# Branch A of the first token block: key blocks of 72 (nine grid rows by eight columns) against key blocks of 128 (sixteen columns by eight rows), with the meta tokens placed apart

## The chip, the cores and the metric

The kernel runs on one core of a Trainium2 chip. The metric is the device time of one execution in microseconds (us). TensorE (PE) multiplies; its weight loads are listed apart as PEld. VectorE is DVE, ScalarE is ACT, GpSimd is POOL, and SyncE (SP) issues the transfers (DMAs).

## The reference, cut to what matters

One encoder layer is applied to two groups of tokens, one sequence of 2048 and one of 512, with 16 learned meta tokens ahead of each.

```
u = rms_norm(h)                                  # 1024 features
qa, ka, va, za, qb, kb, vb, zb, ga, gb = split(u @ w_in)
o_a = neighbourhood_attention(qa, ka, va)        # 8 heads of 64
o_b = window_attention(qb, kb, vb)               # 8 query heads, 2 key heads
y = sigmoid(ga) * ((o_a * silu(za)) @ w_proj_a) + sigmoid(gb) * ((o_b * silu(zb)) @ w_proj_b)
h = h + y @ w_out;  out = rms_norm(h) without the meta tokens
```

Branch A lays the tokens on a grid of 64 columns. The sequence of 512 tokens has 8 rows, so each of its tokens sees all 8 rows, 16 columns around its own, and the 16 meta tokens: 128 + 16 keys under one softmax. All arithmetic is to be as exact as 32-bit floats.

## The kernel before

A 32-bit operand is split in a high part (`h`, a rounded copy by ACT) and a low part (`l`, the rest, by DVE or POOL). A product takes three matmuls, high by high, high by low and low by high; the attention products take two.

**Stages.** The tokens lie in five windows of 512; window 0 is the short sequence, windows 1 to 4 are the long one. The first stage (0 to 126 us) projects window 4 and the meta tokens alone, feature block by feature block (`beside` and `alone`). In the second stage (from 126 us) and the third, two windows share one weight block by a scheme of seven products (`pairs`, `begin`, `sides_first`, `sides`). All projections go to DRAM. From about 990 us on come the attention units, with the remaining gate projections and the output products between them as filling work.

**A unit of branch A.** `unit_a(w, p, h, g)` is one window, one pair of heads, one head and one group of 16 query columns by 8 rows (128 queries). For window 0 a head has four units, g = 0 to 3, and there are eight heads, so 32 units. A unit sees 24 or 32 grid columns. Its keys are a row of meta tokens, written as a ninth row beside the 8 grid rows, so a score tile has 9 x 24 = 216 or 9 x 32 = 288 columns. The steps are: scores (L997, L998), bias and maximum on DVE (L935), exponentials with their sum on ACT (L942), reciprocal and scaling (L946, L953, or on ACT L951 for g = 1), transposes of blocks of 72 keys (8 columns by 9 rows) on PE (L1009), high part by ACT (L1012), low part by DVE (L1013), products with the values (L1024 high, L1026 low). `A_ORDER`, `A_FIRST` and `A_PRODUCTS` say which of the eight column blocks of a head are transposed in which unit and which product covers which groups of queries. A head has 3 + 4 + 4 + 3 = 14 transposes and 6 + 4 + 6 = 16 products, 12 of them over 256 query columns and 4 over 128.

**The values.** `put_v` stores the projected values, transposed, in `va_d`; `put_v_meta` stores those of the meta tokens, from the tile `vm`, in `vrow_d`, which is first filled with zeros. `vm` has one buffer (`bufs=1`). Both are called for the four pairs of heads in the first stage, `put_v_meta` there alone. `put_v` for window 0 runs in the second stage.

**What sets the order.** PE runs in the order in which the program is written, and SP too until the attention begins. On ACT, DVE and POOL a scheduler in the build chooses the order by a simulated timeline. Each engine then runs its list in order, so an instruction that waits holds up all behind it on that engine.

**Names of the second stage's start.** `begin` issues a product into the tile `pa` and one into `pc`; `pairs` then issues `product(a, x["p6"], u[2], False)`, again into `pa`, and `product(e, x["p5"], u[3], True)` into `pe`. The weights `p6` and `p5` are the two halves of a tile `wt` that `sides` makes from two freshly loaded weight tiles: DVE forms `s` (L724, L729, L725, L731), ACT writes the high half (L186) and DVE the low half (L187). `last_operands` splits the operands `u5` and `u6` (L360 on ACT, L361 on DVE). `tq` (L260) is the sum that is stored once `pc` is done.

Of the kernel before, what the change touches and what calls it, by code (L numbers as in the profile page):

```python
# [87 lines left out]
def encoder_block(ctx: ExitStack, tc: tile.TileContext, xT, x_end, w_in, w_pa, w_pb, w_o, norm_g, final_g,  # L88
# [6 lines left out]
    def dt(name, shape):  # L95
        return dram.tile(shape, F32, tag=name, name=name)
# [511 lines left out]
    def put_v(br, w, p, t):  # L608
        vn = ev.tile([P, 2, 4, P], F32R, tag="ev", name="vn")
        transposed(vn, t, 4, P)  # L610
        if br == "a":

            for x in range(2):
                dst = va_d[p][:, w * 64 : (w + 1) * 64, 4 * x : 4 * x + 4].rearrange("g p k f -> p g k f")
                move(dst, vn[64 * x : 64 * x + 64])
        else:
            move(vb_d[w * WTOK : (w + 1) * WTOK].rearrange("(c p) g f -> p g c f", p=P), vn)

    def put_v_meta(br, p, src):
        vm = st.tile([N_META, 2, 1, P], F32R, tag="vm", name="vm", bufs=1)  # L620
        transposed(vm, src, 1, N_META)
        if br == "a":
            if p == 0:
                zr = ev.tile([P, WTOK], F32, tag="t", name="zr", bufs=3)[:, :P]
                nc.vector.memset(zr, 0.0)
                for d in vrow_d:
                    move(d.rearrange("c b g f -> (c b g) f"), zr)
            n = len(META_COLS)
            for y in range(2):
                b = v_block(META_COLS[0] // 8 + y)  # L630
                move(vrow_d[p][:, b : b + n].rearrange("c b g f -> c b (g f)"),
                     vm[8 * y : 8 * y + 8].rearrange("m g o f -> m o (g f)").broadcast_to([8, n, 2 * P]))
        else:
            move(vbm_d, vm[:, :, 0])
# [303 lines left out]
    def sums_of():  # L938
        return at.tile([P, 2], F32, tag="sm", name="sm", bufs=8)
# [22 lines left out]
    def unit_a(w, p, h, g, sh):  # L962

        grows, i0, k0, kr = a_window(w)
        R = kr + 1
        kind = a_kind(w)
        t0 = (0 if w == 0 else DEC_SEQ) + k0 * GRID_W
        nt = kr * GRID_W
        c0, C = CG[g]
        n = R * C  # L970
        nb, kb = C // 8, R * 8
        hs = slice(64 * h, 64 * h + 64)
        qs = slice(g * P, (g + 1) * P)
        if g == 0 and h == 0:
            q = sh["q"] = ld.tile([P, 2, 2, WTOK], F32R, tag="q", name="q")
            move(q.rearrange("p h i t -> p h (i t)"), qa_d[w, p].rearrange("(h d) j x -> (d j) h x", h=2))
        if g == 0 and h == 1:
            z = sh["z"] = ld.tile([P, WTOK], F32, tag="z", name="z")
            move(z, z_d["a", w, p])
        if g == 0:  # L980
            kd = sh["kd"] = ld.tile([P, R, GRID_W], F32R, tag="kd", name="kd")
            move(kd[:, 1:, :].rearrange("p r c -> p (r c)"),
                 ka_d[p][hs].rearrange("d i t -> (d i) t")[:, t0 : t0 + nt])
            move(kd[:, 0, :], kam_d[p][hs].rearrange("d i t -> (d i) t"))
            v = sh["v"] = ld.tile([P, 8, P], F32R, tag="v", name="v", bufs=3)
            move(v[8:kb], va_d[p][h, t0 // 8 : t0 // 8 + kb - 8])
            move(v[:8], vrow_d[p][:, :, h])
            b = sh["b"] = ld.tile([P, a_kind_width(2)], F32, tag="ba", name="ba")
            move(b[:, : a_kind_width(kind)], bias_a[kind][2 * p + h])
        q, kd, v, z, bias = (sh.get(x) for x in ("q", "kd", "v", "z", "b"))  # L990
        yield
        if g == 0 and h == 0:
            sh["y"] = at.tile([P, WTOK], F32, tag="y32", name="y32")
        y32 = sh["y"]
        s = ps_s.tile([P, WTOK], F32, tag="s", name="s")
        sv = s[:, :n].rearrange("p (r c) -> p r c", r=R)
        nc.tensor.matmul(sv, q[:, h, 0, qs], kd[:, :, c0 : c0 + C], start=True, stop=False)  # L997
# [4 lines left out]
        sm = sums_of()[:, :1]  # L1002
        exps(pr[:, :n].rearrange("p (b r c) -> p r b c", b=nb, c=8), sv.rearrange("p r (b c) -> p r b c", c=8), nm, sm)
        yield
        normalise(pr[:, :n], inverse(sm), on_act=g == 1)
# [4 lines left out]
        a = slice(A_FIRST[g], A_FIRST[g] + 2 * nb - 1, 2)  # L1010
        tb = tp[:kb, : nb * P].rearrange("p (b t) -> p b t", t=P)
        nc.scalar.copy(ph_[:kb, a], tb)  # L1012
        nc.vector.tensor_sub(pl_[:kb, a], tb, f32(ph_[:kb, a]))  # L1013
# [4 lines left out]
        for i, (part, b, x, gs) in enumerate(A_PRODUCTS[g]):  # L1018
            vb = v[:kb, v_block(b), :]
            cols = slice(gs[0] * P, (gs[-1] + 1) * P)  # L1020
            src = (ph_ if part == "h" else pl_)[:kb, x : x + len(gs)].rearrange("p b t -> p (b t)")

            if part == "h":
                nc.tensor.matmul(o[:, cols], vb, src, start=g == 1 and i == 0, stop=False, skip_group_check=True)  # L1024
            else:
                nc.tensor.matmul(o[:64, cols], vb[:, :64], src, start=False, stop=(g, i) == (3, 5),  # L1026
                                 skip_group_check=True)
# [511 lines left out]
```

## Time and profile before

| what | us |
|---|---|
| three runs, median (lowest to highest) | 1918.04 (1917.67 to 1918.76) |
| profiled execution, its own time | 1917.62 |
| its span from the first to the last instruction | 1915.5 |
| time around the span | 2.1 |
| PE busy in the span | 1882.1 |
| DVE, ACT, POOL busy | 1313.5, 1143.5, 727.4 |

In the timeline a row gives the start, the duration, and in brackets the idle time before it with what ended it. A matmul's duration covers its way through the pipeline, so the pace of PE is read from one start to the next. ACT and DVE rows overlap by about 0.1 us in the same way. The four units of a head of window 0 return every 11.1 us.

### The profile page before, as it was taken

How to read it: one execution, taken by the hardware profiler on the slowest of the kernel's cores; microseconds unless marked ns; L12 is line 12 of the kernel's file. 1: busy time of each engine (PE TensorE's matmuls, PEld its weight loads, DVE VectorE, ACT ScalarE, POOL GpSimd, SP SyncE). 2: the span in 40 equal slices, each digit the busy share in tenths (PEclk: the TensorE clock that was granted, in tenths of full speed). 3: DMA queues.
4: the chain of work that ended last, by engine and by line, in shares of the span. 5: the costliest groups of instructions: out<-in, count | busy, mean ns of one | idle time of the engine just before them, and what ended most of it. 6: DMA issues, size and time to landing. Idle time of an engine off the chain costs nothing.

```text
span 1915.5 us, 29776 instructions
## 1 busy us (share of the span) xinstructions
PE 1882.1 (98%) x9925; PEld 1599.7 (84%) x9925; DVE 1313.5 (69%) x2899; ACT 1143.5 (60%) x2515; POOL 727.4 (38%) x556
## 2 busy tenths in 40 slices
PE   8999999999999999999999999999999999999998
PEld 6998888888878888888878888888888888888876
DVE  8886445556477544345457788878888887888874
ACT  6454444444464444444456787787788778778831
POOL 2005342323102222323223336646744864684320
PEclk9999999999999999999999999999999999999999
DMA  7667554644296775544369868977986996798482
GB/s 261 218 190 294 175 200 164 220 170 171 90 338 216 240 209 192 193 139 158 110 204 293 255 213 258 303 217 256 306 268 197 305 317 200 234 287 253 129 321 86
DMA packets 223761, 423.78 MB, mean 221 GB/s; under 512 B 49640, under 2 KB 90808, under 8 KB 222072
## 3 DMA queue, kind: packets, MB, share of 16 engines
q1 hardware_dynamic: 223320, 421.88, 67.1%
q8 instruction: 79, 1.29, 0.3%
q14 instruction: 74, 0.61, 0.1%
q10 hardware_dynamic: 288, 0.01, 0.0%
HBM read 303.07 MB, written 118.74 MB: 220 GB/s over the span
## 4 chain that ended last, share of the span: by engine, by line
PE 82%; DVE 5%; ACT 5%; DMA 4%; issue 2%; POOL 1%; SPq 0%; ACTq 0%; DVEq 0%; POOLq 0%
PE pa L758 23%; PE pe L758 11%; PE pc L758 6%; PE mm L137 3%; PE mm L135 3%; PE mm L136 3%; PE tp L1009 3%; PE pso L137 3%; PE pso L135 3%; PE pso L136 2%; PE tp L1109 2%; PE psb L136 2%; PE psb L137 1%; PE oa L1026 1%; PE psb L135 1%
## 5 line engine op out<-in xcount | busy, mean ns | idle before, releaser
L187 POOL TENSOR_TENSOR wt<-wraw,wt 128x512 fp32r<-128x512 f32 x164 | 213.8, 1323 | 271.5 <-ACT wt L186 260.9
L758 PE MATMUL pa<-u,wt 128*128 128x512 f32 x1008 | 242.9, 390 | 0.0
L758 PE MATMUL pa<-u,x 128*128 128x512 f32 x984 | 237.8, 390 | 0.0
L758 PEld LDWEIGHTS pa<-u,wt 128*128 128x128 f32 x1008 | 188.7, 188 | 39.0
L758 PEld LDWEIGHTS pa<-u,x 128*128 128x128 f32 x984 | 183.8, 188 | 38.1
L186 ACT CAST wt<-wraw 128x512 fp32r<-128x512 f32 x312 | 177.6, 618 | 54.9 <-PE mm L137 31.4
L729 POOL TENSOR_TENSOR s<-wraw,raw 128x512 f32<-128x512 f32 x40 | 57.9, 1446 | 273.9 <-DVE x L187 273.9
L135 PE MATMUL mm<-u,wt 128*128 128x512 f32 (+2 forms) x416 | 151.7, 365 | 8.3 <-ACT u L313 7.2
L724 POOL TENSOR_TENSOR s<-raw 128x512 f32<-128x512 f32 x40 | 58.6, 1466 | 255.1 <-DMA raw<-in_w_in_dram 137.6
L137 PE MATMUL mm<-u,wt 128*128 128x512 f32 (+2 forms) x416 | 148.0, 356 | 2.6 <-DVE wt L187 2.0
L136 PE MATMUL mm<-u,wt 128*128 128x512 f32 (+2 forms) x416 | 147.5, 354 | 0.0
L187 DVE TENSOR_TENSOR wt<-wraw,wt 128x512 fp32r<-128x512 f32 x148 | 103.5, 738 | 52.8 <-ACT wt L186 52.4
L758 PE MATMUL pe<-u,wt 128*128 128x512 f32 x504 | 121.8, 391 | 0.0
L758 PE MATMUL pc<-u,wt 128*128 128x512 f32 x504 | 121.1, 389 | 0.0
L1013 DVE TENSOR_TENSOR pl<-tp,ph 128x512 fp32r<-128x512 f32 (+7 forms) x160 | 99.0, 619 | 30.4 <-ACT ph L1012 28.7
L942 ACT ACTIVATE pr<-s,nm 128x384 f32<-128x384 f32 (+5 forms) x160 | 91.2, 570 | 41.2 <-DVE nm L935 40.3
L758 PE MATMUL pe<-u,x 128*128 128x512 f32 x480 | 115.3, 389 | 0.0
L758 PEld LDWEIGHTS pc<-u,wt 128*128 128x128 f32 x504 | 94.6, 188 | 19.6
L758 PEld LDWEIGHTS pe<-u,wt 128*128 128x128 f32 x504 | 94.2, 188 | 19.4
L737 POOL TENSOR_TENSOR s<-wraw,s 128x512 f32<-128x512 f32 x40 | 52.5, 1312 | 145.8 <-DVE wt L187 145.8
L135 PE MATMUL pso<-mh,wt 128*128 128x512 f32 x256 | 107.8, 421 | 0.0
L758 PEld LDWEIGHTS pe<-u,x 128*128 128x128 f32 x480 | 90.1, 188 | 18.7
(237 smaller groups left out, 5035.8 us busy)
## 6 DMA issues: line engine op xcount, KB each, us to landing
wraw<-in_w_in_dram SPq DMA_DIRECT2D x86, 512.0 KB
qa<-evq SPq DMA_DIRECT2D x20, 1024.0 KB
raw<-in_w_in_dram SPq DMA_DIRECT2D x40, 512.0 KB
q<-qa SPq DMA_DIRECT2D x20, 1024.0 KB
wraw<-in_w_o_dram SPq DMA_DIRECT2D x32, 512.0 KB
kbt<-kb SPq DMA_DIRECT2D x32, 384.0 KB
qb<-evq SPq DMA_DIRECT2D x20, 512.0 KB
ka<-evk SPq DMA_DIRECT2D x20, 512.0 KB
```

The source lines that it names most:

```text
L135: nc.tensor.matmul(ps, wh, uh, start=first, stop=False)
L136: nc.tensor.matmul(ps, wh, ul, start=False, stop=False)
L137: nc.tensor.matmul(ps, wl, uh, start=False, stop=last)
L186: nc.scalar.copy(h, r)
L187: low[0] = (eng or lo_eng[0]).tensor_sub(l, r, f32(h)).ins
L724: eng.tensor_add(s1, a21, a22)
L729: eng.tensor_sub(s3, a11, a21)
L737: eng.tensor_sub(s4, a12, s2)
L758: nc.tensor.matmul(ps, wt[:, a, s], u[:, b, kk, :], start=first and kk == 0 and i == 0, stop=kk == 3 and i == 2, skip_group_check=True)
L942: nc.scalar.activation(out, s, AF.Exp, bias=nm, scale=-1.0, accum_out=sm)
L1009: nc.tensor.transpose(tp[:kb, i * P : (i + 1) * P], pr[:, b * kb : (b + 1) * kb], ident)
L1013: nc.vector.tensor_sub(pl_[:kb, a], tb, f32(ph_[:kb, a]))
```

## The change

For window 0 alone the keys are cut in another way. A block of 128 keys is two column blocks of 8 columns by 8 rows. The 16 meta tokens stand in a block of 80 rows of their own (g = 1 and 2, where the other 64 rows are multiplied by zeros) or beside the outermost column block (g = 0 and 3). A head then has 2 + 3 + 3 + 2 = 10 transposes and 4 + 4 + 4 = 12 products, 8 over 256 columns and 4 over 128.

The exponentials are two instructions, one for the grid's keys and one for the 16 meta keys, each with a sum of its own, and DVE adds the two sums. The bias table, the scores and the maximum are as before. In g = 3 the two blocks differ in height, so copy and subtraction are two instructions each.

The values of window 0 get arrays of their own, `va0_d`: two key blocks, then one with the outermost columns, and so on, six blocks of 128 rows for each head. `put_v` writes three pieces for window 0 in place of two. `put_v_meta` writes zeros to four more places (in the first call) and three copies of the meta values more in each call. A unit loads six blocks of 128 (the last three of 80 rows) in place of eight of 72.

```diff
+A0_BEGIN = ((16, 0), (16, 0), (16, 0), (0, 192))
+A0_BLOCKS = (((0, P, 0), (80, P, 1)),
+             ((16, P, 2), (144, P, 4), (0, P, 6)),
...
+A0_PRODUCTS = ((),
+               (("h", 0, P, 1, (0, 1)), ("h", 4, 80, 0, (0,)), ("l", 4, 80, 0, (0,)), ("l", 0, P, 1, (0, 1))),
...
+    va0_d = [dt(f"va0{p}", [2, P, 6, P]) for p in range(4)]
...
-        if br == "a":
+        if br == "a" and w == 0:
+
+            for rows, k, y, b in (slice(64, P), slice(0, 4), 0, 0), (slice(0, 64), slice(1, 4), 64, 0), \
+                    (slice(0, 64), slice(0, 1), N_META, 4):
+                n = k.stop - k.start
+                move(va0_d[p][:, y : y + 64, b : b + n].rearrange("g p k f -> p g k f"), vn[rows, :, k])
+        elif br == "a":
...
+                for d in va0_d:
+                    move(d[:, N_META : N_META + 64, 5].rearrange("g p f -> p g f"),
+                         zr[:64, None, :].broadcast_to([64, 2, P]))
+            for y, b in (0, 4), (64, 3), (0, 5):
+                move(va0_d[p][:, y : y + N_META, b].rearrange("g p f -> p g f"), vm[:, :, 0])
...
-            move(v[8:kb], va_d[p][h, t0 // 8 : t0 // 8 + kb - 8])
-            move(v[:8], vrow_d[p][:, :, h])
+            if w == 0:
+                move(v[:, :3], va0_d[p][h, :, :3])
+                move(v[:80, 3:6], va0_d[p][h, :80, 3:])
...
+        if w == 0:
+            x, xm = A0_BEGIN[g]
+            m0 = META_COLS[(0, 0, 1, 2)[g]] - c0
+            exps(pr[:, x : x + 64 * nb].rearrange("p (b r c) -> p r b c", b=nb, c=8),
+                 sv[:, 1:].rearrange("p r (b c) -> p r b c", c=8), nm, sm[:, :1])
+            exps(pr[:, xm : xm + N_META], sv[:, 0, m0 : m0 + N_META], nm, sm[:, 1:])
+            yield
+            nc.vector.tensor_add(sm[:, :1], sm[:, :1], sm[:, 1:])
+            n = 64 * nb + N_META
...
-        for i, b in enumerate(A_ORDER[g]):
-            nc.tensor.transpose(tp[:kb, i * P : (i + 1) * P], pr[:, b * kb : (b + 1) * kb], ident)
...
+        for i, (x, m, _) in enumerate(blocks):
+            nc.tensor.transpose(tp[:m, i * P : (i + 1) * P], pr[:, x : x + m], ident)
+        for m, i, k, a in places:
+            tb = tp[:m, i * P : (i + k) * P].rearrange("p (b t) -> p b t", t=P)
+            nc.scalar.copy(ph_[:m, a], tb)
+            nc.vector.tensor_sub(pl_[:m, a], tb, f32(ph_[:m, a]))
```

The scheduler's lists differ in two places: in window 0 of branch A (with a few rows of the stage behind it), and from the end of the first stage into the start of the second. On SP at the end of the first stage (the store of the values of the third and fourth pair, `wraw` is the load of a weight tile), before:

```order
L131 DMA wraw_1343<-in_w_in_dram 128x1024
L131 DMA va2_109<-vn_1403 64x2x512 x2
L131 DMA vrow2_113<-vm_1413 8x3x256 x2
L131 DMA wraw_1428<-in_w_in_dram 128x1024
L131 DMA va3_110<-vn_1491 64x2x512 x2
```

and in the changed kernel (`va02` is the new array of the third pair):

```order
L146 DMA wraw_1357<-in_w_in_dram 128x1024
L146 DMA va2_109<-vn_1417 64x2x512 x2
L146 DMA va02_113<-vm_1427 16x2x128 x3
L146 DMA vrow2_117<-vm_1427 8x3x256 x2
L146 DMA wraw_1445<-in_w_in_dram 128x1024
L146 DMA va3_110<-vn_1508 64x2x512 x2
```

Three moves from `vm` stand between the store of the values and the next weight load that did not stand there. On DVE at the change from the first to the second stage, before (`wt_1585` is the tile with p6 and p5, `wraw_1428` the tile loaded last):

```order
L724 TENSOR_TENSOR s_1581<-wraw_1428 128x512
L729 TENSOR_TENSOR s_1582<-wraw_1343,wraw_1428 128x512
L260 TENSOR_TENSOR tkv_1526<-mm_1553,rs4_289 128x256
L700 TENSOR_TENSOR tm_1579<-mm_1553,rs4_289 128x16
L725 TENSOR_TENSOR s_1581<-s_1581,wraw_1343 128x512
L187 TENSOR_TENSOR wt_1585<-s_1581,wt_1585 128x512
L731 TENSOR_TENSOR s_1582<-wraw_1343,s_1581 128x512
L187 TENSOR_TENSOR wt_1585<-s_1581,wt_1585 128x512
L361 TENSOR_TENSOR u5_1628<-x2_347,u5_1628 128x512 x3
L260 TENSOR_TENSOR tq_1622<-pc_1609,s1_1607 128x512
```

and in the changed kernel, where the same tile is `wt_1605`:

```order
L248 TENSOR_TENSOR vm_1518<-vt_1519,vm_1518 16x2x64
L750 TENSOR_TENSOR s_1601<-wraw_1445 128x512
L755 TENSOR_TENSOR s_1602<-wraw_1357,wraw_1445 128x512
L751 TENSOR_TENSOR s_1601<-s_1601,wraw_1357 128x512
L376 TENSOR_TENSOR u5_1648<-x2_351,u5_1648 128x512 x2
L757 TENSOR_TENSOR s_1602<-wraw_1357,s_1601 128x512
L376 TENSOR_TENSOR u5_1648<-x2_351,u5_1648 128x512
L275 TENSOR_TENSOR tq_1642<-pc_1629,s1_1627 128x512
L376 TENSOR_TENSOR u5_1648<-x2_351,u5_1648 128x512
L376 TENSOR_TENSOR u6_1657<-x3_352,u6_1657 128x512 x4
L202 TENSOR_TENSOR wt_1605<-s_1601,wt_1605 128x512 x2
```

The two low halves of the tile moved from ahead of `u5` to behind `tq` and all eight subtractions of `u5` and `u6`. PE, in both kernels, has this order there (names of before):

```order
L758 MATMUL pa_1594<-u0_731,wt_1521 128x512 x12
L758 MATMUL pc_1609<-u1_732,wt_1521 128x512 x12
L758 MATMUL pa_1594<-u2_733,wt_1585 128x512 x12
L758 MATMUL pe_1686<-u3_730,wt_1585 128x512 x12
```

The third of these rows is the first that reads the tile.

## Rows read from the trace of the kernel before

**Rows 1.** The page's busy times, and its chain of waits by engine as shares of the span.

```profile
PE 1882.1 (98%) x9925; PEld 1599.7 (84%) x9925; DVE 1313.5 (69%) x2899; ACT 1143.5 (60%) x2515; POOL 727.4 (38%) x556
...
PE 82%; DVE 5%; ACT 5%; DMA 4%; issue 2%; POOL 1%; SPq 0%; ACTq 0%; DVEq 0%; POOLq 0%
```

**Rows 2.** Busy time of each engine in two head periods of window 0, branch A: length, PE, PEld, DVE, ACT, POOL (instructions in brackets), clock, share of the DMA engines, GB/s.

```profile
1022.20:1033.32 11.12, 11.12 (x70) 9.65 (x70) 8.12 (x25) 7.90 (x20) 5.37 (x4) 1.00 1.05 328
...
1044.44:1055.56 11.12, 11.12 (x70) 9.67 (x70) 8.56 (x22) 7.56 (x19) 5.98 (x5) 1.00 0.75 249
```

**Rows 3.** Timeline of PE in the same stage: start, duration, instruction, count. Four products of 256 columns start at 1033.04, then scores, then three transposes of 72 keys; later four transposes.

```profile
1033.04 0.28 PE L1024 MATMUL oa<-ph,v 72*128 72x256 f32 x1
...
1033.51 0.30 PE L997 MATMUL s<-kd,q 128*128 128x288 f32 x1
...
1033.79 0.49 PE L1009 MATMUL tp<-ident,pr 128*72 128x128 f32 x3
1034.03 0.49 PE L135 MATMUL mm<-u,wt 128*128 128x512 f32 x1
1034.36 0.40 PE L136 MATMUL mm<-u,wt 128*128 128x512 f32 x1
...
1036.33 0.60 PE L1009 MATMUL tp<-ident,pr 128*72 128x128 f32 x4
1036.68 0.48 PE L135 MATMUL mm<-u,wt 128*128 128x512 f32 x1
1037.00 0.39 PE L136 MATMUL mm<-u,wt 128*128 128x512 f32 x1
```

**Rows 4.** Timeline of PE in another window, where a block of keys is 128.

```profile
1326.11 0.49 PE L1009 MATMUL tp<-ident,pr 128*128 128x128 f32 x3
...
1326.68 0.40 PE L136 MATMUL psa<-ya,wt 128*128 128x512 f32 x1
...
1329.04 0.60 PE L1009 MATMUL tp<-ident,pr 128*128 128x128 f32 x4
...
1329.71 0.39 PE L136 MATMUL psa<-ya,wt 128*128 128x512 f32 x1
```

**Rows 5.** Groups of weight loads for the transposes over the span, by shape: count, busy time, mean ns of one, idle before.

```profile
L1009 PEld LDWEIGHTS tp<-ident,pr 128*128 128x128 f32 x224 | 28.4, 140 | 5.7
...
L1009 PEld LDWEIGHTS tp<-ident,pr 128*72 128x72 f32 x112 | 12.3, 114 | 2.6
```

**Rows 6.** Groups by line and shape: count, busy time, mean ns of one, idle before. ACT's copies of 512 and 384 columns and its reading of a sum within 1005 to 1095 us; over the span an ACT instruction of 16 columns and a DVE instruction of one column.

```profile
L1012 ACT CAST ph<-tp 72x512 fp32r<-72x512 f32 x15 | 8.7, 577 | 0.5 <-PE tp L1009 0.2
L1012 ACT CAST ph<-tp 72x384 fp32r<-72x384 f32 x15 | 7.0, 468 | 5.2 <-PE tp L1009 5.2
L942 ACT ACTIVATION_READ_ACCUMULATOR pr<-s,nm 128x1 f32 x28 | 5.4, 193 | 0.0
...
L235 ACT ACTIVATE km<-tm 128x16 fp32r<-128x16 f32 x1 | 0.2, 203 | 0.0
...
L147 DVE TENSOR_TENSOR rs<-rs,rs 128x1 f32<-128x1 f32 x12 | 1.9, 160 | 0.4
```

**Rows 7.** Busy times as in rows 2, at the start of window 0, branch A, and after it.

```profile
1010.00:1015.00 5.00, 4.98 (x33) 4.08 (x32) 2.10 (x7) 2.77 (x7) 1.69 (x2) 1.00 1.04 298
...
1035.00:1040.00 5.00, 5.00 (x32) 4.30 (x32) 4.39 (x11) 3.86 (x10) 2.54 (x2) 1.00 0.47 141
```

**Rows 8.** Timeline of ACT there: the splitting of a loaded weight tile of the gates.

```profile
1012.62 1.14 ACT L186 CAST wt<-wraw 128x512 fp32r<-128x512 f32 x2 [2.21 <-DMA wraw<-in_w_in_dram]
```

**Rows 9.** Timeline of PE at the start of the second stage.

```profile
125.66 2.92 PE L758 MATMUL pa<-u,wt 128*128 128x512 f32 x12
128.41 2.88 PE L758 MATMUL pc<-u,wt 128*128 128x512 f32 x12
131.13 2.88 PE L758 MATMUL pa<-u,wt 128*128 128x512 f32 x12
133.85 2.88 PE L758 MATMUL pe<-u,wt 128*128 128x512 f32 x12
```

**Rows 10.** Timeline of DVE there.

```profile
124.42 0.69 DVE L724 TENSOR_TENSOR s<-wraw 128x512 f32<-128x512 f32 x1 [0.26 <-DMA wraw<-in_w_in_dram]
...
126.88 0.68 DVE L187 TENSOR_TENSOR wt<-s,wt 128x512 fp32r<-128x512 f32 x1
...
131.57 0.68 DVE L260 TENSOR_TENSOR tq<-pc,s 128x512 f32<-128x512 f32 x1
132.17 3.09 DVE L361 TENSOR_TENSOR u<-x,u 128x512 fp32r<-128x512 f32 x5
```

**Rows 11.** Timeline of ACT there.

```profile
128.61 0.59 ACT L769 COPY s<-pa 128x512 f32<-128x512 f32 x1 [0.99 <-PE pa L758]
129.10 4.26 ACT L360 CAST u<-x 128x512 fp32r<-128x512 f32 x8
```

**Rows 12.** Timeline of SP's queue in the last third of the first stage.

```profile
104.10 2.83 SPq L131 DMA_DIRECT2D vrow<-zr  x4
...
118.54 1.65 SPq L131 DMA_DIRECT2D vrow<-vm  x2
120.24 0.36 SPq L131 DMA_DIRECT2D wraw<-in_w_in_dram  x1
```

**Rows 13.** Timeline of ACT there: the first use of `vm` again.

```profile
109.43 0.26 ACT L232 CAST vm<-vt 16x128 fp32r<-16x128 f32 x1 [1.18 <-DMA vrow<-vm]
```

More of the change, by code (lines that the diff above doesn't have):

```diff
@@ L69 @@
                ("h", 6, 12, (2, 3)), ("l", 6, 12, (2, 3))))
+A0_BEGIN = ((16, 0), (16, 0), (16, 0), (0, 192))
+A0_BLOCKS = (((0, P, 0), (80, P, 1)),
+             ((16, P, 2), (144, P, 4), (0, P, 6)),
+             ((16, P, 5), (0, P, 7), (144, P, 9)),
+             ((0, P, 10), (P, 80, 11)))
+A0_PRODUCTS = ((),
+               (("h", 0, P, 1, (0, 1)), ("h", 4, 80, 0, (0,)), ("l", 4, 80, 0, (0,)), ("l", 0, P, 1, (0, 1))),
+               (("h", 1, P, 4, (1, 2)), ("l", 1, P, 4, (1, 2)), ("h", 5, 80, 6, (1, 2)), ("l", 5, 80, 6, (1, 2))),
+               (("h", 2, P, 9, (2, 3)), ("h", 3, 80, 11, (3,)), ("l", 3, 80, 11, (3,)), ("l", 2, P, 9, (2, 3))))
 def v_block(b):
@@ L985, in unit_a @@
             v = sh["v"] = ld.tile([P, 8, P], F32R, tag="v", name="v", bufs=3)
-            move(v[8:kb], va_d[p][h, t0 // 8 : t0 // 8 + kb - 8])
-            move(v[:8], vrow_d[p][:, :, h])
+            if w == 0:
+                move(v[:, :3], va0_d[p][h, :, :3])
+                move(v[:80, 3:6], va0_d[p][h, :80, 3:])
+            else:
+                move(v[8:kb], va_d[p][h, t0 // 8 : t0 // 8 + kb - 8])
+                move(v[:8], vrow_d[p][:, :, h])
             b = sh["b"] = ld.tile([P, a_kind_width(2)], F32, tag="ba", name="ba")
@@ L1001, in unit_a @@
         pr = at.tile([P, 2 * HALF], F32, tag="pr", name="pr", bufs=3)[:, :WTOK]
[L1002 to L1005, printed above, removed]
+        sm = sums_of()
+        if w == 0:
[7 more added lines that the diff above has]
+            n = 64 * nb + N_META
+        else:
+            exps(pr[:, :n].rearrange("p (b r c) -> p r b c", b=nb, c=8), sv.rearrange("p r (b c) -> p r b c", c=8), nm,
+                 sm[:, :1])
+            yield
@@ L1006, in unit_a @@
+        normalise(pr[:, :n], inverse(sm[:, :1]), on_act=g == 1)
         yield
         tp = ps_p.tile([P, WTOK], F32, tag="tp", name="tp")
-        for i, b in enumerate(A_ORDER[g]):
-            nc.tensor.transpose(tp[:kb, i * P : (i + 1) * P], pr[:, b * kb : (b + 1) * kb], ident)
[L1010 to L1013, printed above, removed]
+        if w == 0:
+            blocks = A0_BLOCKS[g]
+            full = [a for _, m, a in blocks if m == P]
+            step = full[1] - full[0] if len(full) > 1 else 1
+            places = [(P, 0, len(full), slice(full[0], full[-1] + 1, step))]
+            places += [(m, i, 1, slice(a, a + 1)) for i, (_, m, a) in enumerate(blocks) if m < P]
+            products = A0_PRODUCTS[g]
+        else:
+            blocks = [(b * kb, kb, None) for b in A_ORDER[g]]
+            places = [(kb, 0, nb, slice(A_FIRST[g], A_FIRST[g] + 2 * nb - 1, 2))]
+            products = [(part, v_block(b), kb, x, gs) for part, b, x, gs in A_PRODUCTS[g]]
@@ L1017, in unit_a @@
         o = sh.get("o")
-        for i, (part, b, x, gs) in enumerate(A_PRODUCTS[g]):
-            vb = v[:kb, v_block(b), :]
+        for i, (part, b, m, x, gs) in enumerate(products):
+            vb = v[:m, b, :]
             cols = slice(gs[0] * P, (gs[-1] + 1) * P)
-            src = (ph_ if part == "h" else pl_)[:kb, x : x + len(gs)].rearrange("p b t -> p (b t)")
+            src = (ph_ if part == "h" else pl_)[:m, x : x + len(gs)].rearrange("p b t -> p (b t)")
             if part == "h":
@@ L1025, in unit_a @@
             else:
-                nc.tensor.matmul(o[:64, cols], vb[:, :64], src, start=False, stop=(g, i) == (3, 5),
+                nc.tensor.matmul(o[:64, cols], vb[:, :64], src, start=False, stop=(g, i) == (3, len(products) - 1),
                                  skip_group_check=True)
```

## The prediction, made before the changed kernel ran

> **What bounds the kernel now.** I read the page's busy times and its chain of waits first. PE is busy for 98% of the span, and 82% of the chain that ended last is PE [rows 1]. So the first question for any edit is how much PE time it removes, and the second is whether it makes PE wait somewhere. The change touches two places, and I read each by itself.
>
> The first place is window 0 of branch A. A head's four units return every 11.12 us there, and in the two head periods shown PE is busy for all 11.12, DVE for 8.1 to 8.6, ACT for 7.6 to 7.9 [rows 2]. PE sets the pace. The reader is to see how dense its starts are: four products over 256 columns take from 1033.04 to 1033.51, which is 0.118 us each [rows 3].
>
> The second place is the passage from the first stage to the second, at 125 to 137 us. PE goes there without a gap from `pa` to `pc`, to `pa` again and to `pe`, one product of twelve matmuls every 2.72 us [rows 9]. In the trace of before both low halves of the tile that the third of these reads are written in good time: the first of them starts on DVE at 126.88 [rows 10], the third product at 131.13.
>
> **The change, part by part: what PE saves.** From the start of three transposes of 72 keys to the second matmul behind them it is 0.57 us (1033.79 to 1034.36), for four it is 0.67 (1036.33 to 1037.00) [rows 3]. One transpose more costs 0.10. A head loses 4 of 14 transposes and 4 of its 12 products over 256 columns: 4 x 0.10 + 4 x 0.118 = 0.87 us. Eight heads give 7.0 us.
>
> The blocks that stay are 128 keys wide where they were 72. In another window, with blocks of 128, the same two distances are 0.57 (1326.11 to 1326.68) and 0.67 (1329.04 to 1329.71) [rows 4]. So a wide transpose goes at the pace of a narrow one, though its weight load takes 140 ns in the place of 114 [rows 5]. I cost the width at nothing; it is hidden because a load runs beside the matmul before it.
>
> A rule of the Trainium skill speaks against this (TensorE: Matmul & The Clock Gate, LDWEIGHTS): a weight load takes a time in proportion to its columns, columns divided by 1.2 in ns. By it the 80 transposes that stay would cost an estimated 47 ns more each, 3.7 us in all. The two pairs of distances above do not show it, so the sum goes without it.
>
> **What ACT and DVE get.** A copy of 512 columns takes 577 ns and one of 384 takes 468 [rows 6], so 0.85 ns a column; I estimate 0.36 us for 256 and 0.25 for 128. A head's copies go from 2 x 0.577 + 2 x 0.468 = 2.09 us to 0.36 + 2 x 0.468 + 2 x 0.25 = 1.80. Four exponentials over 16 columns come in. The trace has none; the nearest ACT row has 16 columns and 203 ns, and the sum is read in 193 ns [rows 6]. So they cost 4 x 0.40 = 1.6 us. ACT comes to about 9.0 us of a new period of 11.12 - 0.87 = 10.25. DVE gets four additions of one column, 0.16 us each [rows 6], and one subtraction more with a quarter fewer columns: about 8.5 to 9.0 us. Both stay below PE, but the way from a unit's scores to its scaled weights grows by 0.56 us, while the units come 0.22 us earlier each.
>
> **What window 0 keeps of the 7.0.** The DMA engines are full at its start, 1.04 at 1010 to 1015 us and still 1.05 in the head period from 1022, and come free by 1035, where the share is 0.47 [rows 2, 7]. ACT stands 2.21 us for a weight tile of the gates until 1012.62 [rows 8]. A transfer that is late does not come earlier because PE is earlier, so what PE has gained by then, some 1.4 heads or 1.2 us, is lost again. For the longer way through ACT and DVE I take off 0.5. The gain is 7.0 - 1.2 - 0.5 = 5.3. Its bounds: 7.0 if nothing is lost. If the three heads under full DMA engines give nothing (2.6 us) and the longer way costs its 0.56 in each of the other five (2.8), 1.6 is left. I stay near the upper end, since the loads of a head go out a whole head ahead.
>
> **What the first stage gets.** This part is about the order, and it is where I expect the gain to go. Each call of `put_v_meta` for branch A now issues five moves out of `vm` in place of two, and the first also four moves of zeros. SP takes 1.65 us for two such moves and 2.83 for four of zeros [rows 12]. SP's list is in order, and the next weight load stands behind them. `vm` has one buffer, so the next `vm` waits until five moves have landed, where it waited for two; even these held up ACT for 1.18 us once, until 109.43 [rows 13]. The load that `s` waits for went out at 120.24 [rows 12], and `s` started at 124.42, with the landing as the end of its wait [rows 10]: 4.2 us. With three moves more ahead of it (2.5 us) it lands at 126.9. If the three of the call before, and the wait for `vm`, push as well, at 129.4.
>
> Now DVE's list. In the changed order `s` (three), `u5` (two), `s`, `u5`, `tq`, `u5`, `u6` (four) come before the low half that the third product needs. Each is 0.6 us (five took 3.09 [rows 10]). The subtractions of `u5` cannot start before ACT has copied, which starts at 129.10 behind the copy of `pa` [rows 11].
>
> - Floor: `tq` waits for `pc`, whose last matmul ends at 128.41 + 2.88 = 131.29 [rows 9]. Then `tq` 0.6, five subtractions 3.0, the low half 0.6: 135.5. The matmul that needs it is the product's third, at 131.13 + 2 x 0.227 = 131.6. PE loses 3.9 us, whenever the load lands.
> - Load at 126.9: three `s` until 128.7, two `u5` from 129.7 to 130.9, `s` 131.5, `u5` 132.1, `tq` 132.7, five until 135.7, low half 136.3. Loss 4.7.
> - Load at 129.4: the same list without the pause ends at 137.8. Loss 6.2.
> - Ceiling: the zeros' 2.8 us push too, and the loss is 9.0.
>
> I take 5.4, between the second and the third. ACT's high halves stand behind eight copies of 4.26 us from 129.10, so they come at about 133.9, before the low half, and add nothing. PE had no gap there, so nothing takes the loss in; all later work follows PE.
>
> The other edits I cost at nothing. The third piece in `put_v` for window 0 is one DMA more in each of four calls in the second stage, behind which PE does not wait. The values' load has 312 KB where it had 288, in two DMAs as before.
>
> **The sum.** 1917.6 (the profiled execution, span 1915.5 and 2.1 around it) + 5.4 - 5.3 = 1917.7. The median of the runs lies 0.4 above that execution, so I predict 1918.1.
>
> **The rivals.**
> - A: the order at the start of the second stage costs nothing, and window 0 gives its share. That is 1918.0 - 5.3 = 1912.7, or 1911.0 with all of the 7.0. For it: DVE waits here and there in that stretch [rows 10], so some work could shift without harm. Against it: `tq` stands ahead of the low half and cannot run before `pc` ends, which is past the moment when PE needs the half.
> - B: window 0 is no longer paced by PE. Its place is ACT, with two exponentials a unit, and the transfers at its start. It decides when a small exponential with its sum takes 0.7 us in place of 0.40, since ACT then has 10.2 us of the 10.25. The gain shrinks to the bound of 1.6, the loss stands at 6.2, and the time is 1918.0 + 6.2 - 1.6 = 1922.6. For it: ACT would be busy for 88% even by my prices. Against it: the loads go out a head ahead.
> - C: wide transposes cost their longer load after all. The loads differ by 26 ns [rows 5], so 80 x 0.026 = 2.1 us, and the time is 1920.2. Against it stand rows 3 and 4.
>
> **How the numbers follow.** Forecast 0.66, A 0.18, B 0.13, C 0.03. The forecast's own range, with losses of 3.9 to 7 and gains of 3.5 to 7.0, is 1915 to 1921.5. The range that I give reaches into A and B: 1912.7 to 1922.5. A measurement of this kernel can tell about 0.2%, 3.8 us, from no change. Faster than 1914.2 are A and a little of the forecast, 0.21. Slower than 1921.8 are most of B and the forecast's upper end, 0.14. Between lies 0.65.
>
> **What would show it.** In the changed profile the twelve matmuls of the second `pa` at 131 us should show a gap of 4 to 6 us that ends with DVE `wt`, and DVE should have `tq` and the eight `u` ahead of it. Head periods of window 0 should be near 10.25 us once the DMA engines come free, with 128-wide transposes 0.10 apart and PE without waits for ACT above 0.5 us. If `pa` runs through without a gap, the forecast is wrong and A holds. If the head periods stay above 10.8, B holds. If they are near 10.5 with no wait of PE, C.

## The result, and the profile after

The changed kernel takes 1925.15 us (median of 6 runs, 1921.06 to 1932.60), the kernel before 1917.86 on the same chip (6 runs, 1916.43 to 1919.68). The ratio is 1.0043, with a 95% interval of 1.0024 to 1.0061: slower, by 0.4%. The prediction was 1918.1 with a range of 1912.7 to 1922.5. It missed, on the side to which it gave 0.14.

The profiled execution took 1927.93 us with a span of 1926.1. Its page, with the busy time of PE, its chain of waits by engine, and the group with the largest idle time of PE's products (the last two columns: idle time before the group, and what ended it):

```profile
PE 1879.7 (98%) x9861; PEld 1594.6 (83%) x9861; DVE 1313.0 (68%) x2939; ACT 1150.0 (60%) x2587; POOL 730.0 (38%) x556
...
PE 76%; DVE 8%; DMA 7%; ACT 4%; POOL 2%; issue 2%; SPq 1%; ACTq 0%; DVEq 0%; POOLq 0%
...
L784 PE MATMUL pa<-u,wt 128*128 128x512 f32 x1008 | 245.4, 392 | 6.5 <-DVE wt L202 3.4
```

PE does 64 instructions less (9925 in [rows 1]), and its part of the chain has fallen from 82% to 76%; DVE and DMA have it now. The third row says where: 6.5 us of idle time in one group of products.

**The start of the second stage.** PE's timeline there, which answers to [rows 9]:

```profile
125.56 2.92 PE L784 MATMUL pa<-u,wt 128*128 128x512 f32 x12
128.32 2.88 PE L784 MATMUL pc<-u,wt 128*128 128x512 f32 x12
134.36 0.73 PE L784 MATMUL pa<-u,wt 128*128 128x512 f32 x2 [3.16 <-ACT wt L201]
138.44 4.63 PE L784 MATMUL pa<-u,wt 128*128 128x512 f32 x10 [3.35 <-DVE wt L202]
142.87 3.08 PE L784 MATMUL pe<-u,wt 128*128 128x512 f32 x12
```

From `pc` to `pe` it was 133.85 - 128.41 = 5.44 us; now it is 142.87 - 128.32 = 14.55. PE loses 9.1 us here. The rows split the loss: the third matmul would have started at 128.32 + 2.72 + 0.45 = 131.49 and starts at 138.44, which is 6.95; and ten matmuls that take 10 x 0.227 = 2.27 at [rows 9]'s pace take 142.87 - 138.44 = 4.43, which is 2.16 more. The windows of this stretch (length, PE, PEld, DVE, ACT, POOL, clock, DMA share, GB/s) show why:

```profile
131.00:134.40 3.40, 0.24 (x2) 0.05 (x1) 3.40 (x7) 3.40 (x8) 0.00 (x0) 1.00 0.99 305
134.40:138.40 4.00, 0.69 (x2) 0.25 (x2) 4.00 (x8) 1.99 (x4) 0.00 (x0) 0.75 0.57 125
138.40:143.00 4.60, 4.56 (x11) 3.59 (x12) 2.40 (x4) 0.00 (x0) 0.00 (x0) 0.50 0.63 202
```

The granted clock falls from 1.00 (2.4 GHz) to 0.50 (1.2 GHz) during the gap, so the ten matmuls behind it go at half pace. Nothing in the prediction stands for this. DVE's timeline tells what PE waited for, as in [rows 10]:

```profile
129.27 0.69 DVE L750 TENSOR_TENSOR s<-wraw 128x512 f32<-128x512 f32 x1 [2.12 <-DMA wraw<-in_w_in_dram]
...
133.49 0.68 DVE L275 TENSOR_TENSOR tq<-pc,s 128x512 f32<-128x512 f32 x1
134.09 3.09 DVE L376 TENSOR_TENSOR u<-x,u 128x512 fp32r<-128x512 f32 x5
137.10 1.28 DVE L202 TENSOR_TENSOR wt<-s,wt 128x512 fp32r<-128x512 f32 x2
```

The load lands at 129.27 (124.42 before), then comes the list that the order showed, and PE goes on at 138.44, when the second of the two low halves is done. ACT's and SP's timelines lead one step further back:

```profile
119.78 0.59 ACT L247 CAST vn<-vt 128x512 fp32r<-128x512 f32 x1 [0.63 <-PE vt L618]
120.27 0.25 ACT L247 CAST vm<-vt 16x128 fp32r<-16x128 f32 x1
```

```profile
121.87 2.54 SPq L146 DMA_DIRECT2D va<-vm  x3
124.45 0.67 SPq L146 DMA_DIRECT2D vrow<-vm  x2
125.17 0.36 SPq L146 DMA_DIRECT2D wraw<-in_w_in_dram  x1
```

The load goes out at 125.17 (120.24 in [rows 12]), behind five moves out of the third `vm`, and ACT writes that `vm` only at 120.27, behind the `vn` of the fourth pair.

**Window 0 of branch A.** Five heads in a row, from the first scores of one head to those of the next:

```profile
1026.60:1036.89 10.29, 10.29 (x60) 8.89 (x61) 8.12 (x29) 8.19 (x31) 4.24 (x4) 1.00 0.97 329
1036.89:1047.42 10.53, 10.53 (x61) 8.88 (x60) 8.91 (x25) 6.81 (x24) 5.22 (x5) 1.00 0.85 288
1047.42:1058.88 11.46, 10.45 (x62) 8.88 (x60) 9.22 (x31) 8.89 (x31) 4.98 (x4) 1.00 0.83 267
1058.88:1069.89 11.01, 10.68 (x61) 8.88 (x60) 8.46 (x29) 7.83 (x29) 5.55 (x4) 1.00 0.59 188
1069.89:1080.11 10.22, 10.22 (x61) 8.82 (x60) 8.05 (x29) 7.67 (x30) 2.60 (x3) 1.00 0.96 337
```

Two heads have the period that PE's count gave (10.25 us), three are longer. The whole of it, as two windows of before and of after (the first three heads, then four):

```profile
993.07:1027.02 33.95, 33.45 (x188) 27.65 (x187) 23.28 (x65) 21.67 (x53) 10.71 (x9) 1.00 0.97 309
1027.02:1071.49 44.47, 44.47 (x273) 38.63 (x272) 33.48 (x91) 29.31 (x73) 18.31 (x15) 1.00 0.78 252
```

```profile
1004.96:1036.89 31.93, 30.81 (x170) 25.69 (x169) 22.17 (x78) 23.68 (x79) 10.69 (x9) 1.00 0.92 305
1036.89:1080.11 43.22, 41.88 (x241) 35.46 (x240) 34.64 (x111) 31.21 (x110) 18.36 (x15) 1.00 0.80 269
```

Seven heads take 75.15 us where they took 78.42, a gain of 3.27. At the prediction's prices (0.10 us for a transpose, 0.118 for a product over 256 columns) 5.4 was there to be had. The four later heads have 16 transposes and 16 such products less, which is 3.48, and keep 1.25. The first window has only 10 transposes and 8 such products less, because those of the last units in it come behind its end; that is 1.94, and it keeps 2.02, all of it. The longest head has one plain wait; PE's and DVE's timelines in it:

```profile
1049.55 0.22 PE L1079 MATMUL oa<-pl,v 80*64 80x128 f32 x1
1050.79 0.33 PE L1079 MATMUL oa<-pl,v 128*64 128x256 f32 x1 [1.01 <-DVE pl L1066]
```

```profile
1049.05 0.91 DVE L285 TENSOR_SCALAR eva<-eva 128x512 f32<-128x512 f32 x1
1049.88 0.38 DVE L961 CUSTOM_DVE_ANT_0 s<-s,ba 128x216 f32<-128x216 f32 x1
...
1050.18 0.55 DVE L1066 TENSOR_TENSOR pl<-tp,ph 128x384 fp32r<-128x384 f32 x1
```

The product waits for a low part that stands on DVE behind a gate's scaling and another unit's maximum. DVE has no pause from 1046.60 to the end of the low part, and two of its scalings are long: the one shown takes 0.91 us and one of 272 columns at 1047.57 takes 0.96, both beside two instructions of POOL that run from 1047.08 to 1049.68. Where POOL is idle, this trace has them at 0.41 to 0.43 and at 0.36. That is 1.1 us more on DVE, as much as PE waits. The place in the list and POOL beside DVE both stand behind this wait, and no run takes them apart. In the head of 11.01 us PE waits 0.33 us for a high part of ACT.

**The rest of the span.** At `pe` the changed kernel is 142.87 - 133.85 = 9.0 us behind the kernel before, at the first scores of window 0 it is 1004.96 - 993.07 = 11.9, seven heads later 1080.11 - 1071.49 = 8.6, and at the end of the span 1926.1 - 1915.5 = 10.6. So about 2.9 us more are lost between the two places and 2.0 behind the second. In the second profile of the same kernel (g3 below) the same two amounts are 1.7 and 1.0. No run was made for them, and their cause is open. The profiled execution is also 2.8 us above the median.

### The profile page after: what moved, and what is told of

Read it like the earlier page. It is cut to its first block, busy times and chain, and to the rows that moved or that the text cites. A ratio compares the mean times of both kernels' runs of the same rounds, so it can differ in the third digit from the quotient of the medians.

```text
span 1926.1 us, 29805 instructions
## 1 busy us (share of the span) xinstructions
PE 1879.7 (98%) x9861; PEld 1594.6 (83%) x9861; DVE 1313.0 (68%) x2939; ACT 1150.0 (60%) x2587; POOL 730.0 (38%) x556
## 4 chain that ended last, share of the span: by engine, by line
PE 76%; DVE 8%; DMA 7%; ACT 4%; POOL 2%; issue 2%; SPq 1%; ACTq 0%; DVEq 0%; POOLq 0%
PE pa L784 20%; PE pe L784 10%; PE pc L784 5%; PE pso L152 3%; PE pso L151 3%; PE pso L150 3%; PE mm L152 2%; PE mm L150 2%; PE mm L151 2%; PE tp L1062 2%; PE tp L1162 2%; PE psb L151 2%; PE psb L152 1%; PE psb L150 1%; DMA wraw<-in_w_in_dram 1%
## 5 line engine op out<-in xcount | busy, mean ns | idle before, releaser
L968 ACT ACTIVATE pr<-s,nm 128x384 f32<-128x384 f32 (+4 forms) x192 | 98.9, 517 | 38.6 <-DVE nm L961 34.8
L1066 DVE TENSOR_TENSOR pl<-tp,ph 128x384 fp32r<-128x384 f32 (+8 forms) x168 | 95.9, 571 | 25.9 <-ACT ph L1065 24.1
```

The source lines that it names most:

```text
L968: nc.scalar.activation(out, s, AF.Exp, bias=nm, scale=-1.0, accum_out=sm)
L1066: nc.vector.tensor_sub(pl_[:m, a], tb, f32(ph_[:m, a]))
```

## The experiments

Eleven kernels ran. "Before" is always the kernel before on the same chip as the kernel it is compared with: 1918.58 us in the first group (e1, e2, e4, e5), 1917.97 in the second (f1 to f4), 1918.34 in the third (g1 to g3).

### e1: the early part alone

On the kernel before, in `put_v_meta`:

```diff
+    va0_d = [dt(f"va0{p}", [2, P, 6, P]) for p in range(4)]
...
+                for d in va0_d:
+                    move(d[:, N_META : N_META + 64, 5].rearrange("g p f -> p g f"),
+                         zr[:64, None, :].broadcast_to([64, 2, P]))
+            for y, b in (0, 4), (64, 3), (0, 5):
+                move(va0_d[p][:, y : y + N_META, b].rearrange("g p f -> p g f"), vm[:, :, 0])
```

> The kernel before, with only the first stage's additions of the change: three more copies of the meta values in each call of put_v_meta and four more moves of zeros in the first. Branch A of window 0 is as before and the new arrays are not read, so the output is the reference's. Theory T (the loss sits at the start of the second stage, window 0 gives back about 3.7 us): the gap in the second pa as in the changed kernel, PE loses 9 to 10 us between 120 and 160 us, time 1926 to 1929 us. Rival W (window 0 is what got slower, the gap is made up for elsewhere): less than 1921 us.

Measured: 1928.22 us, ratio 1.0054 (1.0039 to 1.0069). PE's timeline has the same gap:

```profile
138.28 4.63 PE L764 MATMUL pa<-u,wt 128*128 128x512 f32 x10 [3.09 <-DVE wt L188]
142.72 3.25 PE L764 MATMUL pe<-u,wt 128*128 128x512 f32 x12
```

The added moves and zeros cost 9.6 us, and the gap accounts for 8.9 of them (`pc` at 128.43, so 142.72 - 128.43 - 5.44). Theory T holds, W falls: what made the kernel slower is not in window 0.

### e2: the change without its additions to the first stage

On the changed kernel, with the zeros and copies for `va0_d` taken out of `put_v_meta`; in `put_v` for window 0, beside the zeros:

```diff
+            for j in range(2):
+                for y, b in (8 * j, 4), (64 + 8 * j, 3), (8 * j, 5):
+                    move(va0_d[p][:, y : y + 8, b].rearrange("g c f -> c g f"),
+                         vrow_d[p][:, v_block(META_COLS[0] // 8 + j)])
```

> The changed kernel, with the zeros and the meta copies of the new arrays written in the second stage (in put_v of window 0, from vrow_d), so that SP's and DVE's lists of the first stage are those of the kernel before. Theory T: no gap in the second pa, window 0 gains 3.7 to 5.3 us, time 1912.5 to 1914.5 us, faster than both. Rival W: 1917 us or more. A middle case, in which the moves cost PE something in the second stage: 1914.5 to 1917.

Measured: 1916.48 us, ratio 0.9991 (0.9983 to 1.0000). The second `pa` has no gap, but the middle case came: PE loses time in the second stage. SP spends 6.36 us on six of the copies from DRAM to DRAM from 256.20 on, while a load of `xa` that went out at 253.16 is on its way. From ACT's and PE's timelines:

```profile
261.35 1.06 ACT L470 ACTIVATE xa<-xa 128x1024 f32<-128x1024 f32 x1 [6.73 <-DMA xa<-in_xT_dram]
```

```profile
263.94 4.60 PE L789 MATMUL pa<-u,x 128*128 128x512 f32 x12 [1.91 <-ACT u L800]
```

ACT starts on that load 8.2 us after it went out, in e5, which has no such copies, 5.9 us after (249.56 to 255.50). That the copies hold it up is argued from these rows; it was not tried by itself. Twelve matmuls over 4.60 us are again a stretch of lower clock (0.62 in the mean from 263.94 to 268.38). Where the moves go is thus a question of its own, and e5 answers it better.

### e4: the moves stay, the list is put right

On the changed kernel, in `beside`; `low6` is the subtraction of the low half of `p6`:

```diff
-        with tc.issue_after(copied[0]):
+        with tc.issue_after(low6[0] if wa == 0 else copied[0]):
             for _ in steps:
                 pass
```

> The changed kernel; u5 and u6 may be issued only behind the low half of p6, so the two low halves stand ahead of all eight subtractions on DVE, but still behind tq. All moves and zeros stay, the load is as late as in the changed kernel (lands at about 129.3 us). Theory L (the list is what costs): PE waits 1.5 to 2.5 us in the second pa, the granted clock stays at 1.00, time 1916 to 1919 us. Rival S (the late load is what costs): a gap of 5 us or more and 1922 us or more.

Measured: 1918.22 us, ratio 0.9993 (0.9983 to 1.0003). PE's timeline, and the window behind the second wait:

```profile
131.77 0.73 PE L785 MATMUL pa<-u,wt 128*128 128x512 f32 x2 [0.49 <-ACT wt L201]
133.72 2.55 PE L785 MATMUL pa<-u,wt 128*128 128x512 f32 x10 [1.21 <-DVE wt L202]
136.10 1.07 PE L785 MATMUL pe<-u,wt 128*128 128x512 f32 x4
```

```profile
133.72:136.00 2.28, 2.28 (x10) 1.92 (x11) 2.28 (x5) 0.00 (x0) 0.00 (x0) 1.00 0.88 311
```

The load is as late as in the changed kernel (`s` started at 129.17), and PE loses 136.10 - 128.40 - 5.44 = 2.3 us, at full clock. Theory L holds: with the list put right, `tq` still ahead of the low halves, the late load costs 2.3 of the 9.1 us.

### e5: the zeros alone moved to the second stage

On the changed kernel; these lines go from `put_v_meta` to `put_v` for window 0 and the first pair, with a tile of zeros made there:

```diff
+            if p == 0:
...
+                for d in va0_d:
+                    move(d[:, N_META : N_META + 64, 5].rearrange("g p f -> p g f"),
+                         zr[:64, None, :].broadcast_to([64, 2, P]))
```

> The changed kernel with the four moves of zeros alone put into the second stage; the three moves from vm in each call stay where they are. The scheduler's list there then has the two low halves ahead of u5 again. Theory Z (the zeros are what pushed the loads and turned the list): the load lands at 125 to 126.5 us, PE waits under 1.5 us in the second pa, time 1914 to 1916.5 us. Rival M (the moves from vm push by themselves, through their time on SP and the wait for vm): the load lands at 127 or later, PE waits 2 us or more, time 1918 us or more.

Measured: 1914.32 us, ratio 0.9980 (0.9969 to 0.9990), faster than the kernel before. DVE's and PE's timelines:

```profile
124.95 0.68 DVE L753 TENSOR_TENSOR s<-wraw 128x512 f32<-128x512 f32 x1
```

```profile
129.80 2.88 PE L787 MATMUL pa<-u,wt 128*128 128x512 f32 x12
132.52 2.88 PE L787 MATMUL pe<-u,wt 128*128 128x512 f32 x12
```

The twelve moves out of `vm` are all there, and nothing is lost. Rival M falls. What is left is the gain of window 0, 4.3 us in the medians; in the trace the seven heads take 74.63 us, 3.8 less than before.

### f1: the list alone

On e5, in `beside`; `sides` stops once more ahead of the split of the tile p6/p5, and is taken up again behind `u5` and `u6`:

```diff
             for _ in steps:
                 pass
+            if wa == 0:
+                next(first)
```

> The kernel of e5_zeros_late (loads as early as before: s started at 124.95 us), with the two halves of the tile p6/p5 split only behind u5 and u6, so that ACT's and DVE's lists there are those of the changed kernel. Theory L (the list alone costs most of the gap): ACT's high halves end near 132.8 us, DVE's second low half near 134.9, the second pa resumes there where it needs 130.3: PE loses 4.2 to 5 us, time 1918.5 to 1919.5 us, and 2.3 us more if the granted clock falls to 0.50 behind the gap as in the changed kernel. Rival S (it takes the late load as well): under 1.5 us of gap, 1914 to 1916 us.

Measured: 1919.93 us, ratio 1.0014 (1.0005 to 1.0022). PE's timeline and the window of the ten matmuls:

```profile
132.42 0.73 PE L796 MATMUL pa<-u,wt 128*128 128x512 f32 x2 [2.63 <-ACT wt L201]
134.40 4.15 PE L796 MATMUL pa<-u,wt 128*128 128x512 f32 x10 [1.25 <-DVE wt L202]
138.39 1.99 PE L796 MATMUL pe<-u,wt 128*128 128x512 f32 x8
```

```profile
134.40:138.39 3.99, 3.99 (x10) 3.13 (x11) 2.96 (x5) 0.57 (x2) 0.00 (x0) 0.57 0.42 164
```

With the load on time (`s` at 124.78) the list costs 138.39 - 126.91 - 5.44 = 6.0 us (`pc` started at 126.91): 4.3 of waiting and 1.7 of low clock. Theory L holds with the addition that it had left open, and S falls. Here PE went on after the first low half, so the two halves stand in the other order than in the changed kernel.

### f2: the zeros alone

On the kernel before, in the first call of `put_v_meta`:

```diff
+                for d in va0_d:
+                    move(d[:, N_META : N_META + 64, 5].rearrange("g p f -> p g f"),
+                         zr[:64, None, :].broadcast_to([64, 2, P]))
```

> The kernel before with only the four moves of zeros added; nothing reads what they write and the output is the reference's. The list keeps the two low halves ahead of u5 on DVE, so this is a late load with a good list. Theory Z (the zeros push the loads through SP): s starts at 127.5 to 129 us, and PE loses 0.5 to 2.5 us in the second pa, time 1919 to 1921 us. Rival (the zeros alone make the whole loss): 8 us or more. Rival (the zeros land beside other work and push nothing): s starts before 125.5, no loss.

Measured: 1917.14 us, ratio 0.9997 (0.9987 to 1.0007). Neither theory Z nor the first rival holds; it is the last rival. ACT's timeline:

```profile
117.69 0.26 ACT L233 CAST vm<-vt 16x128 fp32r<-16x128 f32 x1 [0.15 <-DVE wt L188]
...
121.62 0.58 ACT L233 CAST vn<-vt 128x512 fp32r<-128x512 f32 x1
```

The load goes out at 120.60, almost as before, and `s` starts at 124.47. The zeros cost SP 3.4 us at 107 and the queue has made that up by then. So in the first stage the zeros alone cost nothing, the moves alone (e5) cost nothing, and both together cost 9. The rows show the difference: here ACT writes the third `vm` at 117.69, ahead of the fourth `vn`; in the changed kernel it comes at 120.27, behind it. In the changed kernel SP is done with the store of the values at 118.60 + 1.24 = 119.84 and issues the first move out of this `vm` at 121.87. By these rows the late load was itself a matter of the list. This is argued, not shown: no run has both additions and the order of before on ACT. Why the scheduler's order tips when both are there was not tried.

### f3: without the sum over the meta keys

On e5, in `unit_a`:

```diff
-            exps(pr[:, xm : xm + N_META], sv[:, 0, m0 : m0 + N_META], nm, sm[:, 1:])
+            nc.scalar.activation(pr[:, xm : xm + N_META], sv[:, 0, m0 : m0 + N_META], AF.Exp, bias=nm, scale=-1.0)
             yield
-            nc.vector.tensor_add(sm[:, :1], sm[:, :1], sm[:, 1:])
```

> The kernel of e5_zeros_late; in window 0 of branch A the sum over the 16 meta keys and the addition of the two sums are left out, and the scale is sum + 1 in place of its reciprocal (one DVE instruction of one column as before), so the softmax is another. Theory P (the longer way through ACT and DVE is what window 0 does not keep of its 7.0 us): the stalls of PE between 1026 and 1078 us shrink by 1 us or more in all, time 1912.5 to 1913.5 us. Rival D (the transfers at the start of the window are): these stalls stay within 0.5 us, time 1914 to 1915 us.

Measured: 1913.52 us, ratio 0.9978 (0.9969 to 0.9987), an interval that covers e5's ratio. PE's waits between 1026 and 1078 us did not shrink, they moved to other heads (11.22 and 12.46 us, others 10.22 to 10.39): with less to do the scheduler gave another list. The four heads together take 44.29 us, more than e5's 43.24. So neither theory P nor rival D is decided: the work fell and the list changed in one step. For the transfers this experiment says nothing either.

### f4: the gap filled

On the changed kernel, in `pairs` ahead of the second `pa`:

```diff
+                fill = ps_t.tile([P, WTOK], F32, tag="vt", name="fill")
+                for _ in range(24):
+                    nc.tensor.matmul(fill, x["x1"][:, 0, :P], u[2][:, 0, 0, :], start=True, stop=True)
```

> The changed kernel with 24 matmuls of 512 columns more between pc and the second pa, whose result nobody reads; they last 5.4 us and fit in the gap. Theory C (2.3 us of the loss is the half clock that follows the idle time): the ten matmuls behind the gap start at about 138.4 us as in the changed kernel, take 2.3 us from first start to the next product where they took 4.4, the granted clock stays at 1.00, time 2 us below the changed kernel's 1925. Rival (the half clock comes from something else in that stretch): the ten matmuls take 4.4 us again and the time is that of the changed kernel or longer.

Measured: 1921.34 us, ratio 1.0016 (1.0006 to 1.0026). PE's timeline and the last window:

```profile
131.31 5.60 PE L842 MATMUL fill<-u,wt 128*128 128x512 f32 x24
...
137.99 2.58 PE L784 MATMUL pa<-u,wt 128*128 128x512 f32 x10 [0.62 <-DVE wt L202]
140.41 0.84 PE L784 MATMUL pe<-u,wt 128*128 128x512 f32 x3
```

```profile
137.99:140.41 2.42, 2.42 (x11) 1.99 (x12) 2.35 (x4) 0.00 (x0) 0.00 (x0) 1.00 0.27 108
```

The ten matmuls start where they did and take 140.41 - 137.99 = 2.42 us in the place of 4.43, at clock 1.00. Theory C holds in the trace: PE did 24 useless matmuls and needs 140.41 - 128.59 = 11.8 us from `pc` to `pe`, where it needed 14.55 without them. In the medians f4 is 3.4 us above the kernel before, the changed kernel 7.3 and, run again as g3, 4.7; the intervals overlap, so the times by themselves do not show this gain.

### g1 and g2: more filling work between a unit's transposes and its products

On e5, for window 0 of branch A alone (`early`); g1 as shown, g2 with 0.0 and 2.0:

```diff
-            fill(share)
+            fill(share * (0.4 if early else 1))
             next(units[i][2])
-            fill(share)
+            fill(share * (1.6 if early else 1))
```

> The kernel of e5_zeros_late; in window 0 of branch A the filling work between two units is placed 0.4 before and 1.6 behind the transposes in place of 1 and 1. On PE this moves six of the gates' matmuls in each head from ahead of three transposes to behind them, which puts 1.4 us more between a unit's transposes and its products. Theory T (PE waits in window 0 because the copies and low parts of a unit stand too late in ACT's and DVE's lists for its products): the heads that took 11.46 and 11.01 us come down to 10.3 to 10.6, PE loses 1 to 1.7 us less there, time 1912.5 to 1913.5 us. Rival N (then the scaled weights come too late for the transposes, and the wait only moves): the eight heads take as long as before within 0.5 us in all, 1914 to 1916 us.

> As g1_fill_later, with 0 before and 2 behind the transposes: twelve matmuls in each head are moved. Theory T: as g1 or 0.3 us better, 1912 to 1913.5 us. Rival N: waits of the transposes for the scaled weights of the same unit, heads of 11 us and more, 1915 us or more.

Measured: g1 1913.05 us, ratio 0.9973 (0.9961 to 0.9984); g2 1913.36 us, ratio 0.9976 (0.9963 to 0.9989). The four heads of g1 that answer to the last four of the changed kernel above, in one window:

```profile
1023.40:1064.89 41.49, 41.28 (x241) 35.59 (x240) 34.22 (x111) 31.65 (x110) 18.38 (x14) 1.00 0.82 269
```

The heads take 10.23, 10.40, 10.63 and 10.23 us, in all 41.49 where the changed kernel's took 43.22 and before's 44.47: 2.98 of the 3.48 are kept. In the trace the wait shrinks when PE has more to do between a unit's transposes and its products, as theory T has it, and N falls. In the medians g1 lies 1.3 us below e5, which were timed in different groups, and the two intervals overlap; a step of that size is shown by the heads, not by the times. g1 is the best version that ran, 0.27% below the kernel before.

### g3: the changed kernel again

> The changed kernel again, beside the other two on one chip. If its time is the sum of its two parts (the early part alone +9.6 us, the window with the zeros out of the way -4.3), it is 5.3 us above the kernel before, 1922 to 1925 us. If a third part slows it (the first profile had 2.3 us more of waiting between 160 and 980 us, which no other kernel shows), it is 7 to 8 us above.

Measured: 1922.99 us, ratio 1.0026 (1.0015 to 1.0037), 4.7 us above the kernel before. The sum of the parts is 9.6 - 4.3 = 5.3, and these runs need no third part. In the first six runs it was 7.3 us, and the two intervals overlap; the waits of the first profile outside the two places are 2.9 and 2.0 us, so a smaller third part is not ruled out.

## Why the prediction was wrong

**The place was right.** The gap is in the second `pa`, it ends with DVE's `wt`, and `tq` and the eight `u` stand ahead of it. Rival A (the order harmless) falls with that.

**The step that failed is the loss at the start of the second stage: 5.4 us in the sum, 9.1 measured.** Three things stand behind the 3.7.

- The price between the two cases. The load landed as in the third case (129.4 forecast, 129.27 measured), for which the text had worked out 6.2. Taking the middle between the cases for a load that came late cost 0.8. The causes that it named were not quite these: e5 and f2 show that neither the added moves nor the zeros push the load by themselves, and the rows of ACT show the third `vm` behind the fourth `vn`. That the load was late because of this order is argued, as said at f2.
- One low half was counted where the list has two. The matmul started at 138.44, when both were done (137.10 + 1.28). That is 0.6.
- The clock. 2.2 us of the loss are ten matmuls at 1.2 GHz behind the gap; f4 takes them away by keeping PE busy. The prediction counted a gap as if it ended when its cause ends. This is the largest of the three, and no term stood for it, not even in the ceiling of 9.0.

**The gain: 5.3 in the sum, 4.3 in the runs of e5, 3.27 over seven heads in the changed kernel's trace.** The count of PE's savings was right: heads without a wait return after 10.22 and 10.29 us, where 10.25 was forecast, so the 0.87 a head stands, and wide transposes cost nothing (rival C falls). Of the two deductions, the start under full DMA engines was sized too high (1.2; the first three heads kept 2.02 of 1.94, so nothing was lost) and the way through ACT and DVE too low (0.5; the next four lost 3.48 - 1.25 = 2.2). PE waits there for high and low parts between a unit's transposes and its products, and g1 shows that more work for PE in between takes most of it away. Whether the parts are late through their place in the lists, through the longer work that the prediction named, or through POOL beside DVE is open: f3 changed the list too, and no run moved POOL's work.

**Rival B** has a time near the result, 1922.6, but not its reason. A small exponential with its sum takes 0.27 + 0.20 = 0.47 us in the trace (0.40 forecast, 0.7 needed), and ACT is busy for 6.8 to 8.9 us of a head, not 10.2.

**The other edits** were costed at nothing. The third piece of `put_v` costs nothing that a trace shows in e5, which has it. In both profiles of the changed kernel PE waits 0.82 and 0.50 us for ACT's `u` ahead of a product at 382 to 384 us, which e5's does not. This is part of the 2.9 and 1.7 us that are lost between the two places, and what it is stays open.

**The range** ended at 1922.5. The ceiling of the loss (9.0) with the lower gain (1.6) would have given 1925.4, and the text had both numbers. It let the loss go up to 7 in the forecast and set it at 6.2 in B, and put the large loss and the small gain together nowhere.

## What to carry to other kernels

A gap of PE is to be priced with what comes behind it: the next matmuls may go at half the clock, as the ten here did (2.2 us), and useless work for PE can keep them at full clock, as in f4's trace. When a change adds moves ahead of a load, read how the scheduler's lists have moved on every engine that writes what those moves read, and not only on the engine that waits; here two additions, each harmless by itself, went with another list and a late load together. Before giving up a change that is slower, run its parts alone: here most of the gain of window 0 was there, and with four DMAs moved (e5) the kernel is 0.2% faster than before.

## What the runs showed of the hardware

The granted clock fell to 0.50 behind two idle stretches of 3.16 and 3.35 us with two matmuls between them, in f1 behind 2.63 and 1.25 us, and in e2 behind one of 1.91 us; in e4, behind 0.49 and 1.21 us, it stayed at 1.00. The Trainium skill (TensorE: Matmul & The Clock Gate, HAM oscillation — how this bites in real kernels) describes such a case: a wait for data that is long enough puts the array back to the slow clock, and the burst of matmuls behind it starts slow. The trace of the changed kernel agrees, with 4.43 us against 2.27 for the ten matmuls.

A small DVE instruction can last as long as an instruction of POOL. The 32 additions of one column (L1040) take 0.14 to 1.24 us in the changed kernel's trace; all that take more than 0.2 run beside POOL. The longest (DVE's timeline, then POOL's):

```profile
1042.67 1.24 DVE L1040 TENSOR_TENSOR sm<-sm 128x1 f32<-128x1 f32 x1
```

```profile
1041.33 2.57 POOL L202 TENSOR_TENSOR wt<-wraw,wt 128x512 fp32r<-128x512 f32 x2 [0.26 <-ACT wt L201]
```

It ends at 1043.91, and POOL's two at 1043.90. The Trainium skill (SBUF — State Buffer, SBUF: two separate sides) says that DVE and GpSimd share a pair of ports, and that an instruction of DVE with two inputs in SBUF is blocked for the whole of an instruction of GpSimd that reads SBUF and started first. The rows agree. The prediction priced such an addition at 0.16 us, and no term of it took POOL into account.
